# A two-layer hybrid decoder on one core: norm weights loaded in the pair's second block, weight sums a unit later, half-pass chunks a chunk sooner, query blocks scaled a step later

## The chip, the cores and the metric

The kernel runs on one core of one Trainium2 chip. The metric is device microseconds of one execution. Before the change the median of three runs is 1625.3 us (1624.74 to 1626.37). The profile is of one further execution of the same program.

## The reference

Each of two layers normalises x (512 rows of 2048), multiplies by one wide input matrix, sends the columns through three token mixers (retention, differential attention, a gated linear recurrence), multiplies each by a gate, and projects back through one output matrix. The result is normalised and added to x. All is float32. Cut to what matters:

```
for l in range(DEPTH):                                   # 2 layers
    h = rms_norm(x, pre_norm_g[l])
    proj = einsum('bsd,de->bse', h, w_in[l])
    (rq, rk, rv, rg, dq, dk, dv, dg, lx, lg) = split(proj)
    ret_out  = rms_norm(retention(rq, rk, rv)) * silu(rg)
    do       = diff_attention(dq, dk, dv, positions, lam)
    diff_out = rms_norm(do, diff_subln_g[l]) * (1 - lam_init) * silu(dg)
    lru_out  = rg_lru(lx, ...) * silu(lg)
    mixed = concatenate([ret_out, diff_out, lru_out])
    y = einsum('bse,ed->bsd', mixed, w_out[l])
    x = x + rms_norm(y, post_norm_g[l])
```

## The kernel before

**Products.** Every float32 operand is split into a high and a low part, and a product is three matmuls (high by high, high by low, low by high). A weight chunk is 128x1024 (512 KB). SP loads it as `raw` (L182), ACT copies it to `whi` (L190), DVE subtracts to `wlo` (L191). `raw`, `whi` and `wlo` have three buffers each, so a new chunk waits for the matmuls or the split that last used its buffer.

**Passes.** A layer is 13 passes over the input matrix, one pass over the first quarter of the output matrix (pass 13), the Pair, and two half passes (15 and 16) that use two of the four PSUM banks each for the last quarter. While a pass runs, `pump` takes single steps of side tasks (norms, mixers, sums) from a list, one after the other.

**The Pair** (`run_pair`, L321 to L394) computes the second and third quarter of the output in Strassen's way: seven block products, in 28 units of 12 matmuls. The order of units is A11 with chunks 0 to 3, then S1 and S3 by turns, S2 and S4 by turns, A12 and A22 by turns, four chunks each. The left-hand sums are made by `Sums`. The weights' sums are made in `load_unit` (L213 to L243): for S1 a raw chunk is loaded, DVE adds it onto the resident `wx` tiles in two halves (L230), and POOL then sends a DMA that accumulates a further block into the same raw chunk (L234), which S3 splits one unit later. S2 and A22 add a raw chunk onto `wx` in the same way; S4 and A12 use the raw chunk itself.

**Order.** SP's instructions run as the program issues them, one after the other: an issue that waits for a buffer holds all behind it. `ensure` (L246 to L254) issues a chunk's steps ahead of the matmuls: step 0 is issued LOAD = 4 chunks ahead, the rest ADD = 2 ahead or when the chunk is due. The compute engines' order is set by a scheduler with priorities; each engine runs its own list in order too.

**The rest that the change touches.** `load_chunk` (L193 to L210) is the same for the chunks of plain passes. Post-norm weights `pg` (L1186) are loaded by SP at the start of pass 13 (quarter 0), of the Pair (1 and 2) and of pass 15 (3); each takes a tile from a pool of 77. `out_y` (L1015) multiplies an output by them. In `diff_attention` (L674 to L758) a unit is a query block and a head; at a block's last head the block is squared and summed (L738), POOL takes the power (L529), and DVE scales the block (L741, L743). For the next unit DVE takes two masked maxima (L696), negates them (L699), and ACT takes the exponentials (L702).

Of the kernel before, what the change touches and what calls it, by code (L numbers as in the profile page):

```python
# [18 lines left out]
ALU = mybir.AluOpType  # L19
# [16 lines left out]
EPS = 1e-6  # L36
NU = 77
WBUFS = 3
ADD, LOAD = 2, 4
NWARM = 9  # L40
NPOOL = 4
LEAD, SLEAD, RLEAD, NLEAD = 4, 8, 6, 2
# [78 lines left out]
def tile_hybrid_trunk(ctx, tc, x, xt, pos, ppar, lamqk, w_in, gw, w_out, postg, cp, cm, out):  # L121
# [4 lines left out]
    const = ctx.enter_context(tc.tile_pool(name="const", bufs=1))  # L126
    up = ctx.enter_context(tc.tile_pool(name="up", bufs=NU))
    wp = ctx.enter_context(tc.tile_pool(name="wp", bufs=WBUFS))
    tp = ctx.enter_context(tc.tile_pool(name="tp", bufs=8))
    pb = ctx.enter_context(tc.tile_pool(name="pb", bufs=4, space=PSUM))  # L130
    pm = ctx.enter_context(tc.tile_pool(name="pm", bufs=3, space=PSUM))
    pa = ctx.enter_context(tc.tile_pool(name="pa", bufs=1, space=PSUM))
# [41 lines left out]
    chunk_list = []  # L174
    chunk_tiles = {}
    steps = {}
    loaded = [0, 0, 0]
    last_copy = [None]

    def load_raw(src):  # L180
# [12 lines left out]
    def load_chunk(i):  # L193
        p, c = chunk_list[i]
        yield
        yield
        if i:
            raw = load_raw(p.wsrc[c])
            hi, lo = split_tiles()
            split(hi, lo, raw)  # L200
        else:
            src = p.wsrc[0].rearrange("p (k c) -> p k c", k=2)
            raw = wp.tile([P, 2, S], F32, tag="raw", name=nm("raw"))
            hi, lo = split_tiles()
            for a in range(2):
                load_xt(a)
                nc.sync.dma_start(raw[:, a:a + 1, :], src[:, a:a + 1, :])
                split(hi[:, a:a + 1, :], lo[:, a:a + 1, :], raw[:, a:a + 1, :])
        chunk_tiles[i] = (hi, lo)
        yield  # L210


    def load_unit(i):  # L213
        p, (s, c) = chunk_list[i]
        w1, w2 = p.w
        if s == A11_B11:
            src = p.x[c] = [U("wx"), U("wx")]
            for kk in range(2):
                nc.sync.dma_start(src[kk], w1[c][:, kk * S:(kk + 1) * S])
        elif s == S1_T1:  # L220
            p.kept[c] = load_raw(w2[c])
        elif s == S2_T2:
            p.kept[c] = load_raw(w2[c + 4])
        elif s == A12_B21:
            p.kept[c] = load_raw(w1[c + 4])
        yield
        if s in (S1_T1, S2_T2, A22_T4):
            src = p.x[c]
            for kk in range(2):
                V.tensor_tensor(src[kk], src[kk], p.kept[c][:, kk, :], op=ALU.add)  # L230
        elif s != A11_B11:
            src = p.kept[c]
        if s == S1_T1:
            nc.gpsimd.dma_start(p.kept[c], w2[c + 4].rearrange("p (k c) -> p k c", k=2), accum_op=ALU.add)  # L234
        yield
        hi, lo = split_tiles()
        if isinstance(src, list):
            for kk in range(2):
                split(hi[:, kk, :], lo[:, kk, :], src[kk])
        else:  # L240
            split(hi, lo, src)
        chunk_tiles[i] = (hi, lo)
        yield  # L243


    def ensure(i):  # L246
        for step, more in ((0, 0), (1, 0), (2, 0), (0, ADD), (1, ADD), (0, LOAD)):
            while loaded[step] <= min(i + more, len(chunk_list) - 1):
                n = loaded[step]
                if n not in steps:  # L250
                    steps[n] = (load_unit if isinstance(chunk_list[n][0], Pair) else load_chunk)(n)
                with tc.high_priority(HP):
                    next(steps[n])
                loaded[step] += 1  # L254
# [66 lines left out]
    def run_pair(p, begin, loads):  # L321
# [48 lines left out]

        for n, (s, c) in enumerate(UNITS):
            if (s, c) in begin:
                side.append(begin[s, c]())
            if s in SUM_OF:
                until(lambda: (SUM_OF[s], c) in p.sums.parts)
            ensure(base + n + 2)
            hi, lo = chunk_tiles.pop(base + n)
            for t in range(2):
                if c == 0:
                    ps[s, t] = pb.tile([P, S], F32, tag="big", name=nm("big"))  # L380
                for kk in range(2):
                    ah, al = (stationary(s, c, kk, part)[:, t * P:(t + 1) * P] for part in range(2))
                    for m, (wt, at) in enumerate(((hi, ah), (hi, al), (lo, ah))):
                        T.matmul(ps[s, t], lhsT=at, rhs=wt[:, kk, :], start=(c == kk == m == 0),  # L384
                                 stop=(c == 3 and kk == 1 and m == 2))
                if c == 3:
                    held[s][t] = U("held")
                    with tc.high_priority(HP):
                        A.copy(held[s][t], ps.pop((s, t)))
            if n in (11, 19, 27):  # L390
                side.append({11: join_first, 19: join_right, 27: join_left}[n]())
            if n > 11:
                next(loads)
            pump()  # L394
# [279 lines left out]
    def diff_attention(l, st):  # L674
        dv = st["dv"]
        st["dod"] = {}
        units = [(i, h) for i in range(NT) for h in range(DIFF_H)]
        s0s, s1s, wts, accs, pws = {}, {}, {}, {}, {}

        def stage_a(i, h):  # L680
            n = (i + 1) * P
# [39 lines left out]
        def stage_c(i, h):  # L721
# [6 lines left out]
            if h == DIFF_H - 1:  # L728
                o = U("dod")
                V.tensor_copy(o, accs[i])  # L730
                sq = U("dsq")
                A.activation(sq, accs[i], AF.Square)
                ss = tiny("dss", 4)
                V.tensor_reduce(ss, sq.rearrange("p (h e) -> p h e", h=DIFF_H), op=ALU.add, axis=AX.X)
                r0 = tiny("r0", 4)
                V.reciprocal(r0, s0s[i])
                V.tensor_tensor(ss, ss, r0, op=ALU.mult)
                V.tensor_tensor(ss, ss, r0, op=ALU.mult)  # L738
                f = tiny("df", 4)
                rsqrt_mean(f, ss, P, 4)  # L740
                V.tensor_tensor(f, f, r0, op=ALU.mult)  # L741
                o3 = o.rearrange("p (h e) -> p h e", h=DIFF_H)
                V.tensor_tensor(o3, o3, f[:, :, None].to_broadcast([P, DIFF_H, P]), op=ALU.mult)  # L743
                st["dod"][i] = o


        A.activation(ones2, ones, AF.Exp)
# [1 line left out]
        for n in range(len(units) + 2):  # L749
            if n < len(units):  # L750
                stage_a(*units[n])
            if 0 <= n - 1 < len(units):
                stage_b(*units[n - 1])
            if 0 <= n - 2 < len(units):
                stage_c(*units[n - 2])
            yield
            if n < 4 or units[min(n, 15)][0] >= 2:
                yield  # L758

    def evac_dv(st):  # L760
        def f(tb, ps):
# [228 lines left out]
    def load_x(l, st):  # L990
        src = x2 if l == 0 else xs
        for tb in range(NT):
            for n in range(4):
# [2 lines left out]
                st["xr"][tb, n] = t  # L996
                yield

    def squares(st, tbs):
        for t in tbs:  # L1000
            for q in range(4):
# [172 lines left out]
    for l in range(DEPTH):  # L1174
# [5 lines left out]
        for i, (p, tasks) in enumerate(layer_passes[l]):  # L1180
            if i == 13:
                drain()
                side.append(st["sums"].all())
            for n in {13: (0,), 14: (1, 2), 15: (3,)}.get(i, ()):
                st["pg"][n] = U("pg")
                nc.sync.dma_start(st["pg"][n], postg[l, n * S:(n + 1) * S].partition_broadcast(P))  # L1186
            if isinstance(p, Pair):
                run_pair(p, {(S1_T1, 1): st["sums"].rest}, load_x(l, st))
            else:
                run_pass(p)  # L1190
            for t in tasks:
# [98 lines left out]
```

## Time and profile before

| what | value |
|---|---|
| median of the runs | 1625.3 us (1624.74 to 1626.37) |
| the profiled execution, its own time | 1627.36 us |
| its span | 1625.3 us |
| mean granted TensorE clock | 0.997 |
| PE busy | 1607.0 us, 99% |
| DVE busy | 1055.3 us, 65% |
| ACT busy | 713.1 us, 44% |
| POOL busy | 67.5 us, 4% |
| POOL's accumulating loads in layer 0's Pair, issued at | 675.39, 696.07, 697.30, 699.71 us |
| first and last matmul of layer 0's Pair begin | 682.44 and 762.70 us |
| first and last matmul of layer 1's Pair begin | 1489.62 and 1570.88 us |

A row of a timeline has the start in the span, the duration, the engine, the line and the operation, and in brackets the idle time before it with what ended it. A matmul's record is 0.39 us long where the next one starts 0.227 us later, so the records overlap; "PE busy" is therefore no measure of how close TensorE is to its pace, and distances between starts are. In the page's groups the columns are busy time and mean duration, then the idle time before and what ended most of it. A row of the waits has the engine and line that waited, what it waited for, the total, how often, and the longest.

### The profile page before, as it was taken

To read this page: it belongs to the slowest core of one execution; us is meant where nothing else is said; L and a number is where in the kernel's file an instruction comes from. 1 tells how busy PE (TensorE), PEld (TensorE's weight loads), DVE (VectorE), ACT (ScalarE), POOL (GpSimd) and SP (SyncE) were. 2 spreads that over 40 slices of the span, in tenths; PEclk is the share of its full clock that TensorE was granted. 3 is DMA by queue.
4 is the path that set the end of the run, shared out by engine and by line. 5 is a ranking of instruction groups with operands and counts; after the bars stand their busy time and mean duration, and the time that the engine had idled before them with its cause. 6 is when DMAs were issued, how large, how long until landed. Compare 5 with 4: busy or idle time off the path is not lost.

```text
span 1625.3 us, 19623 instructions
## 1 busy us (share of the span) xinstructions
PE 1607.0 (99%) x7445; PEld 1324.6 (81%) x7445; DVE 1055.3 (65%) x1810; ACT 713.1 (44%) x1142; POOL 67.5 (4%) x92
## 2 busy tenths in 40 slices
PE   9999999999999999999999999999999999999997
PEld 7888888888788888877888888887888888888776
DVE  7757756556586556878762774655757644467786
ACT  7233334347742224455752343435673222434452
POOL 1010000000000000000120000000000000000001
PEclk9999999999999999999999999999999999999999
DMA  6423331323232222356743233222323322233566
GB/s 231 125 89 109 95 95 61 92 84 98 78 97 90 87 72 78 116 169 200 227 152 101 92 91 103 66 85 78 98 89 93 104 65 78 91 110 116 150 207 208
DMA packets 57053, 181.70 MB, mean 112 GB/s; under 512 B 6912, under 2 KB 7936, under 8 KB 56960
## 3 DMA queue, kind: packets, MB, share of 16 engines
q1 hardware_dynamic: 53744, 169.94, 32.9%
q0 software_dynamic: 3072, 10.49, 2.5%
q8 instruction: 58, 0.95, 0.2%
q14 instruction: 35, 0.29, 0.1%
q10 hardware_dynamic: 144, 0.04, 0.0%
HBM read 172.05 MB, written 8.39 MB: 111 GB/s over the span
## 4 chain that ended last, share of the span: by engine, by line
PE 91%; DVE 3%; DMA 2%; issue 1%; ACT 1%; POOL 0%; DVEq 0%; POOLq 0%; ACTq 0%
PE big L296 78%; PE big L384 6%; DMA raw<-in_w_out 2%; DVE wlo L191 2%; PE gate L833 1%; PE acc L726 1%; PE ro L927 1%; PE rs L902 1%; PE sc L693 1%; PE sc L694 1%; ACT whi L190 1%; PE wT L716 1%; PE ro L930 0%; PE kv L916 0%; PE hT L1042 0%
## 5 line engine op out<-in xcount | busy, mean ns | idle before, releaser
L191 DVE TENSOR_TENSOR wlo<-raw,whi 128x1024 fp32r<-128x1024 f32 (+1 forms) x281 | 340.8, 1218 | 299.3 <-ACT whi L190 296.8
L190 ACT CAST whi<-raw 128x1024 fp32r<-128x1024 f32 (+1 forms) x281 | 293.4, 1048 | 473.8 <-PE big L296 313.6
L296 PE MATMUL big<-hhi,whi 128*128 128x512 f32 x1024 | 401.9, 393 | 0.0
L296 PE MATMUL big<-hhi,wlo 128*128 128x512 f32 x1024 | 399.1, 390 | 0.0
L296 PE MATMUL big<-hlo,whi 128*128 128x512 f32 x1024 | 399.1, 390 | 0.0
L296 PE MATMUL big<-whi,hhi 128*128 128x512 f32 x640 | 253.4, 398 | 0.0
L296 PE MATMUL big<-wlo,hhi 128*128 128x512 f32 x640 | 249.8, 391 | 0.0
L296 PE MATMUL big<-whi,hlo 128*128 128x512 f32 x640 | 249.8, 390 | 0.0
L296 PEld LDWEIGHTS big<-hhi,wlo 128*128 128x128 f32 x1024 | 192.2, 188 | 40.2
L296 PEld LDWEIGHTS big<-hhi,whi 128*128 128x128 f32 x1024 | 192.4, 188 | 39.6
L296 PEld LDWEIGHTS big<-hlo,whi 128*128 128x128 f32 x1024 | 192.4, 188 | 39.1
L296 PEld LDWEIGHTS big<-wlo,hhi 128*128 128x128 f32 x640 | 120.2, 188 | 25.8 <-DVE wlo L191 0.3
L296 PEld LDWEIGHTS big<-whi,hhi 128*128 128x128 f32 x640 | 120.4, 188 | 24.4 <-ACT whi L190 1.1
L296 PEld LDWEIGHTS big<-whi,hlo 128*128 128x128 f32 x640 | 120.5, 188 | 23.7
L296 PE MATMUL big<-whi,mhi 128*128 128x512 f32 x256 | 100.6, 393 | 0.7 <-ACT whi L190 0.7
L296 PE MATMUL big<-wlo,mhi 128*128 128x512 f32 x256 | 99.8, 392 | 1.0 <-DVE wlo L191 1.0
L296 PE MATMUL big<-whi,mlo 128*128 128x512 f32 x256 | 100.3, 392 | 0.0
L702 ACT ACTIVATE pr<-sc,mx 128x128 f32<-128x128 f32 (+3 forms) x64 | 33.2, 523 | 86.7 <-DVE mx L699 86.7
L296 PEld LDWEIGHTS big<-wlo,mhi 128*128 128x128 f32 x256 | 48.1, 188 | 12.1 <-DVE wlo L191 2.3
L296 PEld LDWEIGHTS big<-whi,mhi 128*128 128x128 f32 x256 | 48.1, 188 | 11.6 <-ACT whi L190 2.0
L296 PEld LDWEIGHTS big<-whi,mlo 128*128 128x128 f32 x256 | 48.1, 188 | 9.7
L384 PE MATMUL big<-whi,sh 128*128 128x512 f32 x128 | 50.7, 396 | 3.0 <-ACT whi L190 3.0
(254 smaller groups left out, 1959.8 us busy)
## 6 DMA issues: line engine op xcount, KB each, us to landing
raw<-in_w_in SPq DMA_DIRECT2D x207, 512.0 KB, 3.6
raw<-in_w_out SPq DMA_DIRECT2D x72, 512.0 KB, 4.1
xT<-in_xt SPq DMA_DIRECT2D x16, 256.0 KB, 6.6
wx<-in_w_out SPq DMA_DIRECT2D x16, 256.0 KB, 5.6
raw<-in_w_out POOLq DMA_DIRECT2D x8, 512.0 KB, 6.2
xr<-in_x SPq DMA_DIRECT2D x16, 256.0 KB, 5.5
xr<-xs SPq DMA_DIRECT2D x16, 256.0 KB, 4.8
pg<-in_postg SPq DMA_DIRECT2D x8, 256.0 KB, 4.1
```

Source lines behind the costliest of these rows:

```text
L190: last_copy[0] = A.copy(hi, raw)
L191: V.tensor_tensor(lo, raw, hi, op=ALU.subtract)
L296: T.matmul(ps[b], lhsT=lhsT, rhs=rhs, start=(cnt[b] == 0), stop=(cnt[b] == total - 1))
L384: T.matmul(ps[s, t], lhsT=at, rhs=wt[:, kk, :], start=(c == kk == m == 0), stop=(c == 3 and kk == 1 and m == 2))
L693: T.matmul(ps[:, :n], lhsT=qs[:, blk], rhs=ks[:, :n], start=True, stop=False)
L694: T.matmul(ps[:, :n], lhsT=qs[:, blk], rhs=kl[:, :n], start=False, stop=True)
L702: A.activation(p[:, :n], sc[c][:, :n], AF.Exp, bias=mx[:, c:c + 1], scale=0.125, accum_out=sums[:, h:h + 1])
L716: T.transpose(ps[:, kb * P:(kb + 1) * P], w[:, kb * P:(kb + 1) * P], ident)
L726: T.matmul(accs[i][:, h * P:(h + 1) * P], lhsT=wt[:, kb * P:(kb + 1) * P], rhs=dv[kb][:, h * P:(h + 1) * P], start=(kb == 0), stop=(kb == i))
L833: T.matmul(ps[:BW, :], lhsT=wt[:BW, cols], rhs=at[:BW, :], start=(n == 0), stop=(n == 2))
L902: T.matmul(ps[:, n * P:(n + 1) * P], lhsT=k[:, n * P:(n + 1) * P], rhs=q[:, n * P:(n + 1) * P], start=True, stop=True)
L927: T.matmul(po[:, n * P:(n + 1) * P], lhsT=sT[:, n * P:(n + 1) * P], rhs=v[:, n * P:(n + 1) * P], start=True, stop=(n == 0))
```

## The change

Four things are changed.

- The weights of quarters 1 and 2 are loaded by a function `load_gain` that the Pair calls at unit S2 with chunk 0 and at S2 with chunk 2, not both before the Pair. Quarters 0 and 3 stay.
- `load_unit` has one step more. S1's add and accumulating load stay in step 1; the adds of S2 and A22 go to step 2, which is issued one unit ahead (NEXT = 1) instead of two.
- `load_chunk` loads the raw chunk of a half pass in step 2, issued a chunk ahead; full passes load in the last step, as before.
- In `diff_attention` the end of a query block becomes a generator `stage_d`: square sum and power in one step, scaling in the next. After the last unit two steps are added for what is left, so that side tasks behind it in the list begin two steps later. The pool of small tiles has 12 buffers instead of 8.

```
-ADD, LOAD = 2, 4
+NEXT, ADD, LOAD = 1, 2, 4
...
-    tp = ctx.enter_context(tc.tile_pool(name="tp", bufs=8))
+    tp = ctx.enter_context(tc.tile_pool(name="tp", bufs=12))
...
     def load_chunk(i):
         p, c = chunk_list[i]
         yield
         yield
+        if len(p.banks) < NT:
+            raw = load_raw(p.wsrc[c])
+        yield
         if i:
-            raw = load_raw(p.wsrc[c])
+            if len(p.banks) == NT:
+                raw = load_raw(p.wsrc[c])
             hi, lo = split_tiles()
             split(hi, lo, raw)
...
     def load_unit(i):
...
         yield
-        if s in (S1_T1, S2_T2, A22_T4):
-            src = p.x[c]
+
+        def add():
             for kk in range(2):
-                V.tensor_tensor(src[kk], src[kk], p.kept[c][:, kk, :], op=ALU.add)
-        elif s != A11_B11:
-            src = p.kept[c]
+                V.tensor_tensor(p.x[c][kk], p.x[c][kk], p.kept[c][:, kk, :], op=ALU.add)
+
         if s == S1_T1:
+            add()
             nc.gpsimd.dma_start(p.kept[c], w2[c + 4].rearrange("p (k c) -> p k c", k=2), accum_op=ALU.add)
         yield
+        if s in (S2_T2, A22_T4):
+            add()
+        yield
+        src = p.x[c] if s in (A11_B11, S1_T1, S2_T2, A22_T4) else p.kept[c]
         hi, lo = split_tiles()
...
     def ensure(i):
-        for step, more in ((0, 0), (1, 0), (2, 0), (0, ADD), (1, ADD), (0, LOAD)):
+        for step, more in ((0, 0), (1, 0), (2, 0), (3, 0), (0, NEXT), (1, NEXT), (2, NEXT), (0, ADD), (1, ADD), (0, LOAD)):
...
             if h == DIFF_H - 1:
                 o = U("dod")
                 V.tensor_copy(o, accs[i])
                 sq = U("dsq")
                 A.activation(sq, accs[i], AF.Square)
-                ss = tiny("dss", 4)
...
-                st["dod"][i] = o
+                ends.append(stage_d(i, o, sq))
+
+        def stage_d(i, o, sq):
+            ss = tiny("dss", 4)
+            V.tensor_reduce(ss, sq.rearrange("p (h e) -> p h e", h=DIFF_H), op=ALU.add, axis=AX.X)
...
+            rsqrt_mean(f, ss, P, 4)
+            yield
+            V.tensor_tensor(f, f, r0, op=ALU.mult)
+            o3 = o.rearrange("p (h e) -> p h e", h=DIFF_H)
+            V.tensor_tensor(o3, o3, f[:, :, None].to_broadcast([P, DIFF_H, P]), op=ALU.mult)
+            st["dod"][i] = o
+            yield
...
                 stage_c(*units[n - 2])
+            if ends and next(ends[0], ends) is ends:
+                ends.popleft()
             yield
             if n < 4 or units[min(n, 15)][0] >= 2:
                 yield
+        while ends:
+            if next(ends[0], ends) is ends:
+                ends.popleft()
+            yield
...
+    def load_gain(l, st, n):
+        st["pg"][n] = U("pg")
+        nc.sync.dma_start(st["pg"][n], postg[l, n * S:(n + 1) * S].partition_broadcast(P))
...
-            for n in {13: (0,), 14: (1, 2), 15: (3,)}.get(i, ()):
-                st["pg"][n] = U("pg")
-                nc.sync.dma_start(st["pg"][n], postg[l, n * S:(n + 1) * S].partition_broadcast(P))
+            if i in (13, 15):
+                load_gain(l, st, 0 if i == 13 else 3)
             if isinstance(p, Pair):
-                run_pair(p, {(S1_T1, 1): st["sums"].rest}, load_x(l, st))
+                run_pair(p, {(S1_T1, 1): st["sums"].rest, (S2_T2, 0): lambda l=l, st=st: load_gain(l, st, 1),
+                             (S2_T2, 2): lambda l=l, st=st: load_gain(l, st, 2)}, load_x(l, st))
```

SP's queue at the start of layer 0's Pair, before; raw_5415 is the raw chunk of S1's chunk 0, the next three raw chunks are those of S1's chunks 1 to 3, and raw_5664 is that of S2's chunk 0:

```order
L182 DMA raw_5415<-in_w_out 128x1024
L1186 DMA pg_5515<-in_postg 128x512
L1186 DMA pg_5517<-in_postg 128x512
L182 DMA raw_5528<-in_w_out 128x1024
L182 DMA raw_5578<-in_w_out 128x1024
L182 DMA raw_5621<-in_w_out 128x1024
L182 DMA raw_5664<-in_w_out 128x1024
```

The same place in the changed kernel:

```order
L182 DMA raw_5415<-in_w_out 128x1024
L182 DMA raw_5524<-in_w_out 128x1024
L182 DMA raw_5574<-in_w_out 128x1024
L182 DMA raw_5617<-in_w_out 128x1024
L182 DMA raw_5660<-in_w_out 128x1024
L182 DMA raw_5704<-in_w_out 128x1024
L182 DMA raw_5750<-in_w_out 128x1024
L1023 DMA pg_5791<-in_postg 128x512
L182 DMA raw_5799<-in_w_out 128x1024
```

The first gain load now follows six more raw chunks, S1's 1 to 3 and S2's 0 to 2; the other one comes eight rows later, between loads of `xr`.

DVE in layer 0's Pair, before, at the splits of S3's chunks 1 and 2 (raw_1035, raw_1045 and raw_1052 hold chunks 1, 2 and 3 of S1 and S3, raw_1061 is S2's chunk 0):

```order
L230 TENSOR_TENSOR wx_999_5364<-wx_999_5364,raw_1052_5621 128x512
L230 TENSOR_TENSOR wx_1000_5365<-wx_1000_5365,raw_1052_5621 128x512
L406 TENSOR_TENSOR sl_1063_5679<-sf_969_5239,sh_1062_5678 128x512
L191 TENSOR_TENSOR wlo_1056_5638<-raw_1035_5528,whi_1055_5637 128x1024
L191 TENSOR_TENSOR wlo_1060_5656<-wx_989_5319,whi_1059_5655 128x512
L191 TENSOR_TENSOR wlo_1060_5656<-wx_990_5320,whi_1059_5655 128x512
L406 TENSOR_TENSOR sl_1067_5699<-sf_991_5335,sh_1066_5698 128x512
L191 TENSOR_TENSOR wlo_1065_5683<-raw_1045_5578,whi_1064_5682 128x1024
L406 TENSOR_TENSOR sl_1072_5725<-sf_1038_5544,sh_1071_5724 128x512
L230 TENSOR_TENSOR wx_967_5223<-wx_967_5223,raw_1061_5664 128x512
L230 TENSOR_TENSOR wx_968_5224<-wx_968_5224,raw_1061_5664 128x512
L191 TENSOR_TENSOR wlo_1069_5703<-wx_999_5364,whi_1068_5702 128x512
```

The same place in the changed kernel (there raw_1033, raw_1043 and raw_1050 hold chunks 1 to 3, and raw_1059 is S2's chunk 0):

```order
L234 TENSOR_TENSOR wx_999_5364<-wx_999_5364,raw_1050_5617 128x512
L234 TENSOR_TENSOR wx_1000_5365<-wx_1000_5365,raw_1050_5617 128x512
L191 TENSOR_TENSOR wlo_1054_5634<-raw_1033_5524,whi_1053_5633 128x1024
L416 TENSOR_TENSOR sl_1061_5675<-sf_969_5239,sh_1060_5674 128x512
L416 TENSOR_TENSOR sl_1065_5695<-sf_991_5335,sh_1064_5694 128x512
L191 TENSOR_TENSOR wlo_1058_5652<-wx_989_5319,whi_1057_5651 128x512
L191 TENSOR_TENSOR wlo_1058_5652<-wx_990_5320,whi_1057_5651 128x512
L416 TENSOR_TENSOR sl_1070_5719<-sf_1036_5540,sh_1069_5718 128x512
L416 TENSOR_TENSOR sl_1074_5741<-sf_1014_5438,sh_1073_5740 128x512
L234 TENSOR_TENSOR wx_967_5223<-wx_967_5223,raw_1059_5660 128x512
L191 TENSOR_TENSOR wlo_1063_5679<-raw_1043_5574,whi_1062_5678 128x1024
L234 TENSOR_TENSOR wx_968_5224<-wx_968_5224,raw_1059_5660 128x512
```

The add of chunk 3 (the first two rows) stands ahead of the split of S3's chunk 1 in both. The add of S2's chunk 0 stood behind the split of S3's chunk 2; half of it now stands ahead of that split. Some twenty rows up, the adds of chunks 1 and 2 stand among A11's splits now, and no longer behind the split of S3's chunk 0. Further on, the splits of S3's chunk 3 and S4's chunk 0 have an add of S2 just ahead, as they had before.

DVE in layer 0's attention where the first query block ends, before (`df` is the power, `dod` the block that is scaled, `mx` the maxima of the next unit):

```order
L528 TENSOR_SCALAR ms_2113<-dss_2106 128x4
L696 ISA sc_2131,mx_2130<-sc_2131,cmt 128x256
L696 ISA mx_2130 128x1
L741 TENSOR_TENSOR df_2112<-df_2112,r_374_2108 128x4
L696 ISA sc_2134,mx_2130<-sc_2134,cmt 128x256
L696 ISA mx_2130 128x1
L743 TENSOR_TENSOR dod_2102<-dod_2102,df_2112 128x512
L699 TENSOR_SCALAR mx_2130<-mx_2130 128x2
```

And in the changed kernel:

```order
L538 TENSOR_SCALAR ms_2113<-dss_2106 128x4
L706 ISA sc_2129,mx_2128<-sc_2129,cmt 128x256
L706 ISA mx_2128 128x1
L706 ISA sc_2132,mx_2128<-sc_2132,cmt 128x256
L706 ISA mx_2128 128x1
L756 TENSOR_TENSOR df_2112<-df_2112,r_374_2108 128x4
L709 TENSOR_SCALAR mx_2128<-mx_2128 128x2
L758 TENSOR_TENSOR dod_2102<-dod_2102,df_2112 128x512
```

The second maximum now stands ahead of the instruction that waits for the power, and the negation ahead of the scaling. In the half pass ACT's split of pass 15's chunk 1 (L190) stood behind four copies of the Pair's banks (L389) and three squares (L1008); now it stands behind one copy.

More of the change, by code (lines that the diff above doesn't have):

```diff
@@ L176, in tile_hybrid_trunk @@
     steps = {}
-    loaded = [0, 0, 0]
+    loaded = [0, 0, 0, 0]
     last_copy = [None]
@@ L372, in run_pair @@
             if (s, c) in begin:
-                side.append(begin[s, c]())
+                task = begin[s, c]()
+                if task is not None:
+                    side.append(task)
             if s in SUM_OF:
@@ L677, in diff_attention @@
         units = [(i, h) for i in range(NT) for h in range(DIFF_H)]
-        s0s, s1s, wts, accs, pws = {}, {}, {}, {}, {}
+        s0s, s1s, wts, accs, pws, ends = {}, {}, {}, {}, {}, deque()
         def stage_a(i, h):
@@ L732, in stage_c @@
                 A.activation(sq, accs[i], AF.Square)
-                ss = tiny("dss", 4)
[L734 to L743, printed above, removed]
-                st["dod"][i] = o
+                ends.append(stage_d(i, o, sq))
+        def stage_d(i, o, sq):
+            ss = tiny("dss", 4)
+            V.tensor_reduce(ss, sq.rearrange("p (h e) -> p h e", h=DIFF_H), op=ALU.add, axis=AX.X)
+            r0 = tiny("r0", 4)
+            V.reciprocal(r0, s0s[i])
+            V.tensor_tensor(ss, ss, r0, op=ALU.mult)
+            V.tensor_tensor(ss, ss, r0, op=ALU.mult)
+            f = tiny("df", 4)
+            rsqrt_mean(f, ss, P, 4)
[5 more added lines that the diff above has]
+            yield
         A.activation(ones2, ones, AF.Exp)
```

## Prediction

> **What bounds the kernel now.** I read the first part of the page, then the shares of the chain that ended last, then what TensorE waited for.
>
> ```profile
> span 1625.3 us, 19623 instructions
> PE 91%; DVE 3%; DMA 2%; issue 1%; ACT 1%; POOL 0%; DVEq 0%; POOLq 0%; ACTq 0%
> PE big L384 <- ACT whi L190: 3.0, 2, 2.1
> PE big L384 <- DVE wlo L191: 2.5, 4, 1.2
> PE big L296 <- DVE wlo L191: 1.0, 3, 0.5
> PE sc L693 <- ACT pr L702: 0.8, 2, 0.4
> PE big L296 <- ACT whi L190: 0.7, 3, 0.3
> ```
>
> TensorE makes the time: 91% of the last chain is its own work, and no edit here touches a matmul. Only its waits can be had (columns: total, times, longest). 5.5 us of them stand in the Pair (L384), 1.7 us in passes (L296), 0.8 us in the scores of the attention (L693). A wait understates its loss, because the row's length overlaps the next start; so I count starts. Timeline of PE, the Pair of both layers:
>
> ```profile
> 682.44 0.39 PE L384 MATMUL big<-whi,mhi 128*128 128x512 f32 x1
> 699.89 0.39 PE L384 MATMUL big<-wlo,sh 128*128 128x512 f32 x1
> 701.25 0.39 PE L384 MATMUL big<-wlo,sh 128*128 128x512 f32 x1
> 702.55 0.50 PE L384 MATMUL big<-whi,sh 128*128 128x512 f32 x1 [0.91 <-ACT whi L190]
> 703.81 0.50 PE L384 MATMUL big<-wlo,sh 128*128 128x512 f32 x1 [0.53 <-DVE wlo L191]
> 762.92 0.39 PE L296 MATMUL big<-whi,mhi 128*128 128x512 f32 x1
> 1489.62 0.39 PE L384 MATMUL big<-whi,mhi 128*128 128x512 f32 x1
> 1510.94 0.80 PE L384 MATMUL big<-whi,sh 128*128 128x512 f32 x1 [2.12 <-ACT whi L190]
> 1571.11 0.39 PE L296 MATMUL big<-whi,mhi 128*128 128x512 f32 x1
> ```
>
> From 682.44 to 699.89 lie 77 steps of 0.2266 us: the undisturbed pace. The Pair has 336 matmuls, so 76.1 us. From its first matmul to pass 15's first it took 80.48 us (layer 0) and 81.49 us (layer 1): it lost **4.3 and 5.4 us**. The first long stall of layer 0 is 701.25 to 702.55, less one step: 1.07 us. Two things lie behind it, on SP's timeline and in the chain of waits:
>
> ```profile
> 657.82 0.33 SPq L182 DMA_DIRECT2D raw<-in_w_out  x1
> 686.65 1.87 SPq L1186 DMA_DIRECT2D pg<-in_postg  x2
> SPq L1186 <- DVE y L1015: 56.9, 2, 28.4
> 701.45 1.05 ACT whi L190
> 703.78 5.88 DMA raw<-in_w_out
> 715.16 3.15 DMA raw<-in_w_out
> 1504.18 5.59 DMA raw<-in_w_out
> ```
>
> SP stands 28.4 us (56.9 in both layers) in front of the two gain loads, until pass 13's last y gives a tile back. Behind them in its order are the raw chunks of S1, which so start at 688.6 (686.65 + 1.87) instead of about 663. Their adds, and the accumulating loads that POOL sends after them, come late by the same; the accumulate at 1504.18 is the piece that ends just before layer 1's stall of 2.12 us.
>
> **The change part by part.**
>
> The **gain loads** go behind six raw loads (order rows of SP in the section on the change). S1's chunks 1 and 2 then need only a raw buffer, at about 663 and 668 by my estimate (buffers free as units' splits end, some 5 us apart). Their adds need the chunk of wx split, 684 to 688; accumulates go out there instead of at 696 to 700, and land before 695. The chunk of S3 that stalled at 702.55 has its data 7 us early. Its wlo stands behind the add of chunk 3, as before; that chunk's raw needs the buffer that S3's chunk 0 gives back at its split, 692.9. With the slow landing of 5.88, two adds and a split it ends by 692.9 + 5.9 + 1.3 + 1.2 = 701.3, with 701.95 wanted (unit 7's start 682.44 + 7 × 2.72, and two matmuls). Both first stalls go, and with layer 1's its slow clock. What these cost beside idle time:
>
> ```profile
> 703.00:709.00 6.00, 5.47 (x25) 4.33 (x24) 1.00 0.91 229
> 1509.00:1515.00 6.00, 4.02 (x10) 2.79 (x11) 0.72 1.04 212
> L191 DVE TENSOR_TENSOR wlo<-raw,whi 128x1024 fp32r<-128x1024 f32 (+1 forms) x281 | 340.8, 1218 | 299.3 <-ACT whi L190 296.8
> L230 DVE TENSOR_TENSOR wx<-wx,raw x48: 681/686/695, 673.5 to 1558.3; 128x512 f32<-128x512 f32 x48
> ```
>
> In the windows of the Pair's matmuls the granted clock (after the two busy times) is 1.00 after layer 0's stall and 0.72 after layer 1's; the eight starts behind 1510.94 are late by 1.9 us together. I tie these to the stall before them. The Trainium skill, "TensorE: Matmul & The Clock Gate", section "Part 1: The HAM clock gate (the "warmup" mystery)", has half rate only after about 3.4 us of idleness, in a window that runs freely. Here 2.1 us of idleness were enough, so the trace speaks against that length. By the page's rule the 1.9 us would not hang on this stall, and the sum below would be 9.3 in place of 11.2.
>
> The **later adds** of S2 and A22 stand a unit further back. This is free if raw chunk, add and split keep up with TensorE's 5.45 us for two units. A raw buffer is freed by a split, its next load takes 3.15 (alone) to 5.88 us (beside an accumulate), then half an add or both (0.6 or 1.2) and the next split of 1.22: 5.0 to 8.3 us. Only S2's first chunks can meet an accumulate, that of chunk 3 at about 699. For S3's chunk 2 I get 700 + 4.5 + 0.6 + 1.2 = 706.3, 707.4 wanted; with 5.88 it is 707.7, a stall of 0.3. The next load starts there; if it too takes 5.88, its round ends at 715.4 with 713.2 wanted, 2.2 more; if it takes 3.15, at 712.7, nothing. Bounds: 0 to 2.5 us a layer; I take 0.6, nearer to the free end, because after that one accumulate the loads are alone and the row of 3.15 is theirs. It can't be below nothing: the pace is 0.2266 already.
>
> On the rule of DMA: the 5.88 us stand beside accumulates by POOL, 3.15 alone. The Trainium skill, "DMA: Bandwidth & Descriptors", section "SWDGE vs HWDGE vs iDMA", says that software and hardware descriptors feed different internal queues of an engine, which takes turns between them. That speaks against the change, which puts raw loads beside accumulates; the row agrees. If every load of S2 met one, the third rival's time would result.
>
> The **half pass** (chunk loads a chunk sooner, and their split above the Pair's last copies in ACT's order rows):
>
> ```profile
> 765.42 0.39 PE L296 MATMUL big<-wlo,mhi 128*128 128x512 f32 x1
> 766.03 0.50 PE L296 MATMUL big<-whi,mhi 128*128 128x512 f32 x1 [0.22 <-ACT whi L190]
> 766.82 0.40 PE L296 MATMUL big<-whi,mlo 128*128 128x512 f32 x1
> 767.48 0.50 PE L296 MATMUL big<-wlo,mhi 128*128 128x512 f32 x1 [0.26 <-DVE wlo L191]
> 1575.67 0.50 PE L296 MATMUL big<-wlo,mhi 128*128 128x512 f32 x1 [0.24 <-DVE wlo L191]
> 761.03 0.57 ACT L389 COPY held<-big 128x512 f32<-128x512 f32 x1
> ```
>
> Lost: 0.61 − 0.23 = 0.38 and 0.66 − 0.23 = 0.43, and by an equal wait (1575.67) the same in layer 1: **1.6 us**. ACT held this split back behind four copies and three squares; now one copy is ahead, so it needs only its buffer and by my estimate ends some 4 us sooner than 766.0, against a wait of 0.2. The copies that fall behind it are later by one split of ACT (some 1.05 us, the row at 701.45); the first of their banks was free at 761.6 and is wanted six matmuls behind pass 15's first, at 764.3. The last pass's own stalls at the program's end (the third of "x3" in both rows) keep their order and stay.
>
> The **query block's scaling**:
>
> ```profile
> 258.05 0.39 PE L296 MATMUL big<-hlo,whi 128*128 128x512 f32 x1
> 258.85 0.38 PE L693 MATMUL sc<-st,st 128*128 128x256 f32 x1 [0.42 <-ACT pr L702]
> 255.97 1.02 POOL df L529
> 257.58 0.55 DVE dod L743
> 258.12 0.09 DVE mx L699
> PE rsb L587 <- DVE rb L586: 0.3, 1, 0.3
> PE gate L833 <- ACT xh L818: 0.2, 1, 0.2
> ```
>
> DVE waited for POOL's power (to 257.0) ahead of the second maximum, then scaled 0.55 us, then negated the maximum that ACT's exponential needs. In the new order both maxima stand before that wait and the negation before the scaling: it moves from 258.1 to about 257.2, 0.9 us, against 0.80 − 0.23 = 0.57 us lost, once a layer ("0.8, 2" in the waits above): **1.15 us**. Two added steps at the attention's end push gates and heads back by 24 matmuls, 5.4 us. The largest waits of PE for gates and heads are 0.3 and 0.2 us (last two rows); I cost the shift at nothing, and such a wait gone or come at ± 0.5. Tables on ACT go from 26 loads to 22, beside idle time.
>
> **Sum**: 4.3 + 5.4 + 1.6 + 1.15 = 12.4, less 2 × 0.6 left in S2: **11.2 us**. The profiled execution took 1627.4 us in all (2.1 around its span), so 1616.2 for it; the median of the runs, 1625.3, is 2.1 below it, so **1614.1**.
>
> **The rivals.**
>
> 1. The loop of raw load, add and split binds in S2. For it: 5.88, and stalls that layer 0 had behind the first, which sum to 4.3 − 1.07 = 3.2. Against: one accumulate only is left there. At its upper bound of 2.5 us a layer the gain is 12.4 − 5.0 = 7.4: 1617.9.
> 2. The gain loads only move the wait: the new place waits for a tile too, and holds what is queued behind. For it: 28.4 us for a tile at the old place. Against: pass 13's last y is by then 10 us past. The Pair then keeps its 9.7, and 1.6 + 1.15 = 2.8 remain: 1622.5, which is within 0.2%.
> 3. Slower. The adds of late raw chunks stand ahead of the splits of S3 on DVE, as its order rows show, and DVE can't pass them. If each of chunks 1 to 3 lands as slowly as the row of 5.88, a round takes 0.03 + 5.9 + 1.2 + 1.2 = 8.3 against 5.45: 2.9 × 3, less some 2.2 of slack, 6.5 a layer, and a slow clock of 1.9 with it: 8.4 a layer for the 4.3 and 5.4 lost now, +7.1, less 2.8: 1629.6. It costs more than before from a landing of 5.2 us in all three: 3 × (5.2 − 3.0) − 2.2 + 1.9 = 6.3 a layer, half of the 12.4 now lost. Against: chunks 1 and 2 have 20 us more to land, and only one accumulate is left beside the rest.
> 4. The clock falls in the Pair whatever the stall (the page's rule, above): 1.9 less: 1616.0. For it: only 2.1 us of idleness came before. Against: layer 0, 1.00 with its 0.9 and 0.5 us.
>
> **How the numbers follow.** Forecast (1612.5 to 1615.7) 0.53, rival 4 0.05, rival 1 (to 1619.5) 0.22, rival 2 0.08, rival 3 0.05; 0.07 for something between 1619.5 and 1622. The range of 8 in 10 reaches from the lower bound (nothing left in S2, and 0.5 of side work: 1614.1 − 1.7) to rival 1's with a slow clock of 1.9 on top: 1612.4 to 1619.8. Within 0.2% (3.25 us) is about what a measurement here can't tell from none, so faster is below 1622.05: 0.86; same 0.09; slower 0.05.
>
> **What would show it.** SP's gain loads after S2's start, raw loads of S1's chunks 1 and 2 before 672; POOL's accumulates before 690; the stalls at 702.5 and 1510.9 gone with a clock of 1.00; the waits L296 by one each; the L693 row gone; the Pair 76.2 to 77.5 us long. Wrong would be: a wait by DVE for a raw chunk ahead of an S3 split (rival 1 or 3), a stall that reappears in the gates and heads which moved 5.4 us.

## The result

Four runs of the changed kernel have a median of 1616.15 us (1615.81 to 1617.22), four of the kernel before 1625.84 us (1624.74 to 1627.07): a ratio of 0.9941 with a 95% interval of 0.9924 to 0.9959. That is 9.7 us, or 0.6%, faster. Forecast were 1614.1 us and a gain of 11.2 us. The time lies in the stated range, 2 us above the forecast.

### The profile page after: what moved, and what is told of

The parts are those of the page before. It is cut to its first block, busy times and chain, and to the rows that moved or that the text cites. A ratio compares the mean times of both kernels' runs of the same rounds, so it can differ in the third digit from the quotient of the medians.

```text
span 1613.8 us, 19637 instructions
## 1 busy us (share of the span) xinstructions
PE 1602.5 (99%) x7445; PEld 1324.9 (82%) x7445; DVE 1053.7 (65%) x1810; ACT 709.1 (44%) x1138; POOL 67.6 (4%) x92
## 4 chain that ended last, share of the span: by engine, by line
PE 95%; DVE 2%; DMA 1%; ACT 1%; issue 1%; POOL 0%; DVEq 0%; POOLq 0%; ACTq 0%
PE big L304 79%; PE big L394 8%; PE gate L855 1%; DVE wlo L191 1%; PE acc L736 1%; DMA raw<-in_w_out 1%; PE ro L949 1%; PE rs L924 1%; PE sc L703 1%; PE sc L704 1%; PE ro L952 0%; PE kv L938 0%; PE wT L726 0%; PE hT L1068 0%; PE rT L979 0%
## 5 line engine op out<-in xcount | busy, mean ns | idle before, releaser
L191 DVE TENSOR_TENSOR wlo<-raw,whi 128x1024 fp32r<-128x1024 f32 (+1 forms) x281 | 341.4, 1218 | 285.7 <-ACT whi L190 282.8
L190 ACT CAST whi<-raw 128x1024 fp32r<-128x1024 f32 (+1 forms) x281 | 293.7, 1048 | 468.4 <-PE big L304 305.2
L304 PE MATMUL big<-hhi,whi 128*128 128x512 f32 x1024 | 401.9, 393 | 0.0
L304 PE MATMUL big<-hlo,whi 128*128 128x512 f32 x1024 | 399.4, 390 | 0.0
L304 PE MATMUL big<-hhi,wlo 128*128 128x512 f32 x1024 | 399.0, 390 | 0.0
L304 PE MATMUL big<-whi,hhi 128*128 128x512 f32 x640 | 253.5, 398 | 0.0
L304 PE MATMUL big<-whi,hlo 128*128 128x512 f32 x640 | 249.9, 391 | 0.0
L304 PE MATMUL big<-wlo,hhi 128*128 128x512 f32 x640 | 249.7, 391 | 0.0
L304 PEld LDWEIGHTS big<-hhi,whi 128*128 128x128 f32 x1024 | 192.4, 188 | 40.6 <-ACT qk L680 0.9
L304 PEld LDWEIGHTS big<-hhi,wlo 128*128 128x128 f32 x1024 | 192.2, 188 | 40.2
L304 PEld LDWEIGHTS big<-hlo,whi 128*128 128x128 f32 x1024 | 192.4, 188 | 38.7
L304 PEld LDWEIGHTS big<-wlo,hhi 128*128 128x128 f32 x640 | 120.2, 188 | 25.7
L304 PEld LDWEIGHTS big<-whi,hhi 128*128 128x128 f32 x640 | 120.5, 188 | 23.9 <-ACT whi L190 0.7
L304 PEld LDWEIGHTS big<-whi,hlo 128*128 128x128 f32 x640 | 120.6, 188 | 23.8
L304 PE MATMUL big<-wlo,mhi 128*128 128x512 f32 x256 | 100.2, 392 | 0.5 <-DVE wlo L191 0.5
L304 PE MATMUL big<-whi,mhi 128*128 128x512 f32 x256 | 100.3, 392 | 0.1
L304 PE MATMUL big<-whi,mlo 128*128 128x512 f32 x256 | 100.2, 391 | 0.0
L304 PEld LDWEIGHTS big<-wlo,mhi 128*128 128x128 f32 x256 | 48.1, 188 | 10.9 <-DVE wlo L191 1.0
L304 PEld LDWEIGHTS big<-whi,mhi 128*128 128x128 f32 x256 | 48.1, 188 | 10.2 <-ACT whi L190 0.5
L304 PEld LDWEIGHTS big<-whi,mlo 128*128 128x128 f32 x256 | 48.1, 188 | 9.7
L190 ACT CAST whi<-wx 128x512 fp32r<-128x512 f32 x64 | 37.1, 619 | 38.8 <-PE big L394 28.8
```

The lines of the kernel that those rows point to most:

```text
L190: last_copy[0] = A.copy(hi, raw)
L191: V.tensor_tensor(lo, raw, hi, op=ALU.subtract)
L304: T.matmul(ps[b], lhsT=lhsT, rhs=rhs, start=(cnt[b] == 0), stop=(cnt[b] == total - 1))
```

## The profile after

The profiled execution took 1615.81 us with a span of 1613.8 us; the one before took 1627.36 us. The page, the chain's shares and all that TensorE waited for in passes, Pair and scores:

```profile
span 1613.8 us, 19637 instructions
PE 95%; DVE 2%; DMA 1%; ACT 1%; issue 1%; POOL 0%; DVEq 0%; POOLq 0%; ACTq 0%
PE big L304 <- DVE wlo L191: 0.5, 1, 0.5
PE big L394 <- DVE wlo L191: 0.4, 1, 0.4
PE sc L703 <- ACT pr L712: 0.3, 2, 0.2
```

Lines have moved: L394 is the Pair (L384 before), L304 the passes (L296), L703 the scores (L693), L182 and L191 are as they were. The Pair's waits went from 5.5 us in six waits to one of 0.4, the passes' from 1.7 to 0.5 (the program's last pass), the scores' from 0.8 to 0.3. Timeline of PE around the Pairs:

```profile
682.25 0.39 PE L394 MATMUL big<-whi,mhi 128*128 128x512 f32 x1
707.72 0.50 PE L394 MATMUL big<-wlo,sh 128*128 128x512 f32 x1 [0.38 <-DVE wlo L191]
759.38 0.39 PE L304 MATMUL big<-whi,mhi 128*128 128x512 f32 x1
1484.63 0.39 PE L394 MATMUL big<-whi,mhi 128*128 128x512 f32 x1
1560.81 0.39 PE L304 MATMUL big<-whi,mhi 128*128 128x512 f32 x1
```

First matmul to pass 15's first is 77.13 us in layer 0 (80.48 before) and 76.18 in layer 1 (81.49), against 76.15 at the undisturbed pace. From profile to profile the Pairs gave 3.4 and 5.3 us. What SP and POOL issued in layer 0's Pair:

```profile
657.63 55.46 SPq L182 DMA_DIRECT2D raw<-in_w_out  x7
713.14 0.42 SPq L1023 DMA_DIRECT2D pg<-in_postg  x1
686.01 0.90 POOL L238 DMA_DIRECT2D raw<-in_w_out  x1 [9.73 <-ACT whi L190]
688.37 0.87 POOL L238 DMA_DIRECT2D raw<-in_w_out  x1 [1.47 <-ACT whi L190]
697.89 0.87 POOL L238 DMA_DIRECT2D raw<-in_w_out  x1 [8.65 <-ACT sh L415]
```

The gain load stands behind seven raw loads and waits for nothing worth a row; the accumulates of chunks 1 and 2 start at 686 and 688 instead of 696 and 697, that of chunk 3 at 698 instead of 700.

## The experiments

Each was made from the kernel before (the first four) or from the changed one, with five rounds against the kernel before; runs of one group shared a chip. Before had a median of 1624.71 us in the first group, 1625.46 in the second, 1625.70 in the third.

### The four parts, each alone

```
 # e1_gain: kernel before, and
-            for n in {13: (0,), 14: (1, 2), 15: (3,)}.get(i, ()):
+            if i in (13, 15):
+                load_gain(l, st, 0 if i == 13 else 3)
...
+                run_pair(p, {(S1_T1, 1): st["sums"].rest, (S2_T2, 0): lambda l=l, st=st: load_gain(l, st, 1),
+                             (S2_T2, 2): lambda l=l, st=st: load_gain(l, st, 2)}, load_x(l, st))
 # e2_adds: kernel before, and in load_unit
+        if s in (S2_T2, A22_T4):     # in a step of its own, a unit later
+            add()
 # e3_half: kernel before, and in load_chunk
+        if len(p.banks) < NT:
+            raw = load_raw(p.wsrc[c])
+        yield
 # e4_diff: kernel before, and diff_attention of the changed one, with 12 small tiles
```

> Only the gain loads move (into S2); adds, half passes and attention as before. Theory: SP's 28 us wait before S1's raw chunks is the cause of the first long stall of each Pair. S1's raw loads start before 672 us, the stalls at 702.5 (2.0 us with what follows it) and 1510.9 (2.4, and 1.9 of slow clock) are gone, the later ones of 715 to 739 stay: Pair of layer 0 78.4 us long (80.5 before), of layer 1 77.2 (81.5). Time 4.4 us below before where before's execution had no slow clock (median about 1621.4), 6.3 below where it had one. Rival: the order of the adds on DVE binds and the waits only come back one chunk later; then the Pairs stay within 0.7 us of 80.5 and 81.5 and the time within 1.5 us of before.

> Only the adds of S2 and A22 come a unit later; the gain loads stay before the Pair. Theory: the first long stall of each Pair stays (702.5 and 1510.9, SP blocked for 28 us), at most the later ones go: gain between 0 and 2 us. Rival: the adds are what shortens the Pair, SP's wait was hidden: Pairs of 77.1 and 76.2 us as with the whole change, gain about 7 us.

> Only the half-pass chunks are loaded a chunk sooner. Theory: the four stalls at 766.0, 767.5, 1574.2 and 1575.7 go, 1.6 us, and the Pairs stay at 80.5 and 81.5 us: 1624.2 against 1625.8. Rival: ACT's order there came from the Pair's earlier end and not from this edit; then the four stalls stay and the gain is under 0.3 us.

> Only the query block's end is a step later. Theory (from the profile of the whole change): the wait of the score matmuls falls from 0.8 to 0.3 us in total, since the negated maximum still stands behind the instruction that waits for POOL's power: gain 0.5 us, not 1.15. Rival of the prediction: both stalls go entirely, gain 1.15 us. A third: the shift of gates and heads by 24 matmuls costs or brings over 0.5 us by itself, visible in stalls between 345 and 425 and between 1110 and 1185 us.

| run | median us | ratio to before | Pair, layer 0 and 1, in its profile |
|---|---|---|---|
| gain loads alone | 1619.14 | 0.9964 (0.9951 to 0.9976) | 77.2, 77.4 us |
| later adds alone | 1625.42 | 1.0002 (0.9993 to 1.0011) | 79.6, 79.2 us |
| half passes alone | 1622.86 | 0.9985 (0.9976 to 0.9994) | 80.0, 80.0 us |
| query blocks alone | 1624.71 | 0.9997 (0.9988 to 1.0007) | 79.2, 80.0 us |

The gain loads are the larger part of the change: alone they bring 0.36 of 0.59%, and the Pairs fall to 77.2 and 77.4 us (78.4 and 77.2 were expected). In layer 0 that is more than expected: the later stalls between 715 and 739, which were to stay, are gone as well. In the profile of the later adds alone SP stands before the gain loads as it did, and the chain of waits has the same pieces, raw landing, adds, accumulate, split, up to the stall:

```profile
659.55 0.33 SPq L182 DMA_DIRECT2D raw<-in_w_out  x1
688.39 1.86 SPq L1008 DMA_DIRECT2D pg<-in_postg  x2
1496.71 6.03 DMA raw<-in_w_out
1502.77 1.30 DVE wx L231 x2
1504.62 5.15 DMA raw<-in_w_out
1509.85 1.05 ACT whi L190
```

The rows are SP's timeline and, from 1496 on, the chain. Without the gain loads' move the later adds bring nothing that the runs can tell; the interval ends 1.1 us below before, far from the rival's 7. The half passes alone lose the four stalls, as their waits show (of the three waits in each row of L296 one is left, that of the last pass), and bring 1.9 us (interval 1.0 to 3.9) where 1.6 was summed:

```profile
PE big L303 <- DVE wlo L191: 0.5, 1, 0.5
PE big L303 <- ACT whi L190: 0.4, 1, 0.4
```

The query block's edit more than halves the waits, alone as in the whole (0.8 to 0.3 us in all); in time it can't be told from nothing, nor from the 1.15 us of the prediction. Multiplied, the four ratios give 0.9948, so no large interaction is needed for the whole's 0.9941.

### The whole again, and without the later adds

```
 # e5_whole: the changed kernel.   e6_no_adds: the changed kernel, and in load_unit
-        if s == S1_T1:
+        if s in (S1_T1, S2_T2, A22_T4):
             add()
...
-        if s in (S2_T2, A22_T4):
-            add()
```

> The whole change again, beside the next three on one chip. Theory (the parts seen apart: gain loads 5.6, half passes 1.9, attention 0 to 0.5, later adds nothing alone): 8 to 10 us below before. The prediction's 11.2 holds the 1.9 us of slow clock that only some executions of before have. Rival: 11.2 us, the parts simply worth what the one profile showed.

> The whole change without the later adds (S2 and A22 as before). Theory: once the gain loads are out of the way, the later adds are worth the stalls that the gain loads alone left at 709.8 (0.8) and 1513.8 (1.1): 0.5 to 2 us slower than the whole change, Pairs of about 77.2 and 77.4 us. Rival: the adds' place does nothing; then the same as the whole change within 0.3 us, and the Pairs 77.1 and 76.2.

The whole: 1616.75 us, ratio 0.9948 (0.9935 to 0.9960), 8.7 us below before, as expected; the interval, 6.5 to 10.6 us, leaves out the rival's 11.2. Without the later adds: 1616.71 us, 0.9944 (0.9931 to 0.9958), with Pairs of 77.3 and 76.2 us (77.4 and 76.3 in the whole of this group). My theory fell: the later adds make no difference that the runs can tell, neither alone nor on top; the intervals leave room for some 2 us, but the Pairs agree within 0.1. DVE has the same order here: the add of S2's chunk 0 begins at 706.25, the split of S3's chunk 2 behind it at 706.86, and TensorE stalls at 708.13 as in the whole. The stall of 1.1 us that the gain loads alone had left in layer 1 is not there, though the adds are issued as they were: so it is not due to their place. What made it stays open.

### What is left in layer 0: hold the accumulate, or take the adds off DVE

Chain of the changed kernel before the stall at 707.72, then DVE's timeline there:

```profile
697.27 1.23 DVE wlo L191
698.52 7.30 DMA raw<-in_w_out
706.45 1.23 DVE wlo L191
705.84 0.69 DVE L234 TENSOR_TENSOR wx<-wx,raw 128x512 f32<-128x512 f32 x1 [3.73 <-DMA raw<-in_w_out]
706.45 1.22 DVE L191 TENSOR_TENSOR wlo<-raw,whi 128x1024 fp32r<-128x1024 f32 x1
```

S2's chunk 0 is loaded at 698.52, just behind the accumulate that POOL sent at 697.89, and takes 7.30 us. Its add stands at DVE's head for 3.73 us; the split of S3's chunk 2 stands behind it. Two edits separate landing and order.

```
 # e7_hold: the changed kernel, and in load_unit, S1's chunk 3 accumulates only after this
+            zero, one = tiny("hold", 1), p.kept[3][:, 0, :1]
+            G.tensor_tensor(zero, p.kept[0][:, 0, :1], p.kept[0][:, 0, :1], op=ALU.subtract)
+            G.tensor_tensor(one, one, zero, op=ALU.add)
 # e8_both: as e7_hold, and e9_behind: the changed kernel, each with this in stage_d
-            V.tensor_tensor(f, f, r0, op=ALU.mult)
+            V.scalar_tensor_tensor(r1, newest[0][:, :1].to_broadcast([P, 4]), 0.0, r0, op0=ALU.mult, op1=ALU.add)
+            V.tensor_tensor(f, f, r1, op=ALU.mult)
 # e10_pool_adds: as e9_behind, and in load_unit for S2 and A22
-            add()
+            add(G)
```

> The whole change, with the accumulating load of S1's chunk 3 held back on POOL until S2's chunk 0 has landed (POOL adds a difference of that chunk with itself, zero, to one column of the other first). Theory: the 7.3 us landing of S2's chunk 0 in layer 0 comes from the accumulate beside it; it falls to 3.2 to 4.0, the stalls at 707.7 and 735.2 (0.9 us) go, layer 0's Pair is 76.2 to 76.5 us long, gain 0.6 to 0.9 us on the whole change. Rival: the landing is slow for another reason (its issue, the splits): it stays above 5.5 us and the Pair at 77.1; or the accumulate, now later, keeps S3's chunk 3 waiting and costs over 0.5 us.

> As the run before, and the factor of a query block is tied behind the negated maximum of the next unit (zero times that maximum is added to it), so that the negation no longer stands behind the wait for POOL's power. Theory: the two score stalls left (0.32 us each) go too: 0.6 us below the run before, 1.2 to 1.6 below the whole change. Rival: the place of the score matmuls on TensorE sets the stall, and it stays at 0.3 each; or the four added instructions a layer cost as much.

> The whole change, and the factor of a query block is tied behind the next unit's negated maximum (zero times that maximum is added to it); no hold on the accumulate. Theory: the two score stalls of 0.32 us go, 0.6 us below the whole change (1616 to 1616.8): 1615.4 to 1616.2. Rival: the run before won its 1.1 us by chance of the clock; then no difference from the whole change, with the stalls gone or not.

> As the run before, and the adds of S2 and A22 run on POOL instead of DVE. Theory: the stall of layer 0's Pair that the whole change leaves (0.5 to 0.9 us at 707.7) comes from the add of S2's chunk 0 that stands at the head of DVE, waiting for a raw chunk that lands late beside the accumulate, while the split of S3's chunk 2 behind it is ready since 702.3. Without that add on DVE the stall goes, the landing of 6 to 7 us stays: Pair of layer 0 76.2 to 76.4 us, 0.9 us more gained. Rival: POOL's adds take so long, or slow DVE so much, that S2's or A22's own splits come late: Pairs of 77.5 us or more.

**Holding the accumulate** gave 1620.67 us, 0.9970 (0.9959 to 0.9982): 3.9 us slower than the whole. The rival's second half came: the later accumulate keeps S3's chunk 3 waiting. Layer 0's Pair is 79.9 us long where 76.2 to 76.5 were expected. Its chain:

```profile
699.97 4.73 DMA raw<-in_w_out
706.90 6.68 DMA raw<-in_w_out
713.68 1.05 ACT whi L190
714.76 1.24 DVE wlo L191
```

Without the accumulate beside it the raw chunk lands in 4.73 us instead of 7.30 (3.2 to 4.0 were expected), and the stall at 707.7 is gone. So the hold took 2.6 us off the landing; why it still takes 4.73 us and not 3.15, as a load alone in the prediction, stays open. The accumulate itself, sent at 706.90, takes 6.68 us and now makes S3's chunk 3 late: 1.2 and 0.7 us of stall at 714.8 and 716.0, and a slow clock behind them (0.79 from 716 to 724).

**The negation freed** from the wait for POOL's power. On top of the hold: 1619.61 us, 0.9964 (0.9951 to 0.9976), 1.1 below it, which the intervals don't tell apart. On the whole change alone: 1616.42 us, 0.9946 (0.9933 to 0.9958), where the whole had 0.9948. The row of the scores is gone from the waits of both profiles; the 0.6 us that the two stalls had lost is too little to be told in time from the whole change.

**The adds on POOL** gave 1620.54 us, 0.9971 (0.9960 to 0.9983), 4.1 us slower than the run beside it that has the adds on DVE. The rival came: the Pairs are 80.3 and 78.4 us long (77.7 and 76.2 beside it). The stall at 707.7 is gone: without the add at its head DVE splits S3's chunk 2 at 702.16, right behind ACT's copy, and not at 706.45. That shows that the add's place made that stall, and not the chunk's own data. But POOL takes 1.80 us for an add that takes DVE 0.69, and DVE's own work beside it slows down. POOL's adds are busy until 742.1, a new stall of 2.4 us by starts ends at 742.7 with a slow clock behind it, and a like one of 2.1 us comes in layer 1. DVE's timeline at that split, the group of POOL's adds, then DVE's timeline before the new stall, and the stall:

```profile
702.16 1.23 DVE L191 TENSOR_TENSOR wlo<-raw,whi 128x1024 fp32r<-128x1024 f32 x1 [0.17 <-ACT whi L190]
L234 POOL TENSOR_TENSOR wx<-wx,raw 128x512 f32<-128x512 f32 x32 | 56.8, 1800 | 29.9 <-DMA raw<-in_w_out 17.6 <-PE big L394 7.9 <-DVE held L351 2.4
737.51 1.77 DVE L191 TENSOR_TENSOR wlo<-wx,whi 128x512 fp32r<-128x512 f32 x1
739.21 1.78 DVE L357 TENSOR_TENSOR held<-held,held 128x512 f32<-128x512 f32 x1
742.57 0.68 DVE L358 TENSOR_TENSOR held<-held,held 128x512 f32<-128x512 f32 x1
742.70 0.50 PE L394 MATMUL big<-wlo,mhi 128*128 128x512 f32 x1 [2.23 <-DVE wlo L191]
```

No version beat the whole change by a margin that the runs can tell.

### Two more profiles of the kernel before

Nothing is edited; each is one look at the kernel before.

> The kernel before once more, unchanged, for a second profile of it. Theory: the stall that starts layer 1's trouble at 1510.9 is there again (1.3 to 2.3 us), but the slow clock behind it (1.9 us) comes only in some executions and in others falls elsewhere or nowhere; the Pair of layer 1 is then some 79.6 us long. Rival: it belongs to the stall and is there each time: 81.5.

> The same once more: a third profile of the kernel before. Expected as in the run before it.

| profile of before | time us | Pair layer 0 | Pair layer 1 | first stall of layer 1 |
|---|---|---|---|---|
| first (of the prediction) | 1627.36 | 80.48 us | 81.49 us | idle 2.12 us |
| second | 1626.09 | 79.76 us | 79.85 us | idle 1.00 and 0.53 us |
| third | 1625.56 | 80.48 us | 80.07 us | idle 1.25 and 0.53 us |

The theory fell, though not to the rival either: the slow clock in layer 1's Pair is in all three, as windows around it show (first, second, third; then layer 0's first stall in the second; then layer 1's stretch in the changed kernel):

```profile
1509.00:1517.00 8.00, 6.02 (x19) 4.42 (x20) 4.77 (x6) 5.74 (x9) 0.00 (x0) 0.79 0.95 217
1509.00:1517.00 8.00, 6.47 (x20) 4.55 (x19) 5.62 (x8) 5.79 (x9) 0.00 (x0) 0.79 0.96 239
1509.00:1517.00 8.00, 6.23 (x20) 4.64 (x20) 5.69 (x8) 5.83 (x9) 0.00 (x0) 0.79 0.95 241
703.00:709.00 6.00, 4.53 (x19) 3.44 (x20) 4.77 (x6) 5.67 (x9) 0.00 (x0) 1.00 0.98 231
1503.00:1511.00 8.00, 8.00 (x37) 6.63 (x36) 5.16 (x8) 3.59 (x5) 0.00 (x0) 1.00 0.54 136
```

The columns are the window, its length, the busy times of PE, PE's loads, DVE, ACT and POOL, then the granted clock (0.79 three times, then 1.00), the DMA share and GB/s. What varied were the stalls: 81.49 us was the longest of three Pairs, the others are 1.6 and 1.4 us shorter. The first stall makes 0.4 and 0.2 of that (by starts it lost 2.28, 1.86 and 2.11 us), and 0.7 is a further stall that only the first profile has:

```profile
1546.95 0.50 PE L384 MATMUL big<-wlo,sh 128*128 128x512 f32 x1 [0.56 <-DVE wlo L191]
```

Nor is the slow clock there whenever the stall is: the profiles of the later adds alone and of the query blocks alone have the stall in layer 1 (2.3 and 2.1 us lost) and a clock of 1.00 behind it.

## Why the prediction was right, and where it was off

**The gain loads** (4.3 and 5.4 us of the sum): right in mechanism and place. SP's raw loads run from 657.6, the accumulates of chunks 0 to 2 have gone out by 688.4, both first stalls and layer 1's slow clock are gone. Of the sum's terms this one was mis-sized most: the 5.4 us of layer 1 were those of one execution, with a longer first stall and a further one at 1546.95. The two later profiles of before lose 79.85 − 76.15 = 3.7 and 3.9 us there. With 3.8 in place of 5.4 the sum is 9.6 us, with the query block's 0.5 in place of 1.15 (below) 9.0; the gains measured by medians are 9.7 and 8.7 us (the whole, twice), with intervals of some 2 to 3 us on either side. The step that carried it over was "so 1616.2 for it; the median of the runs, 1625.3, is 2.1 below it, so 1614.1": the profiled execution of before was the longest of the runs then known, and its long Pair of layer 1 was counted whole as gain. From profile to profile the fall was 11.5 us; the kernel's was less.

**The later adds**: costed at a loss of 0 to 2.5 us a layer, 0.6 taken. What is left in the Pairs is 1.0 us in layer 0 and nothing in layer 1, 1.0 in all against 1.2. But that loss is not theirs: it stays when the adds go back to their old place, so that the sizes match is luck. The cause is the one named, a raw load beside an accumulate (7.30 us, more than the 5.88 that was the upper bound), at the place named, S3's chunk 2, and it is the third rival's mechanism in one chunk: an add at the head of DVE before a split that is ready. The prediction had named just this, a wait by DVE for a raw chunk ahead of an S3 split, as a sign of being wrong; it came, but in one layer and for 0.5 to 1.1 us in the profiles of the whole and of its variants that keep this order, not for the rival's 6.5 and more.

**The half passes** (1.6 us): right. In the whole and alone all four stalls are gone.

**The query block** (1.15 us): the direction was right, the size less than half: the stalls fell by 0.5 us in all, and the row of the scores, which was to be gone, stayed with 0.3. The order was read on DVE alone. The negation did move 0.9 us forward, but the score matmuls moved too: before, 1,073 matmuls of the passes stand ahead of the one that stalls in layer 0, now 1,070, three steps of 0.227 us sooner. Timeline of PE and DVE after:

```profile
257.22 0.39 PE L304 MATMUL big<-hlo,whi 128*128 128x512 f32 x1
257.77 0.38 PE L703 MATMUL sc<-st,st 128*128 128x256 f32 x1 [0.16 <-ACT pr L712]
256.87 0.16 DVE L756 TENSOR_TENSOR df<-df,r 128x4 f32<-128x4 f32 x1 [0.44 <-POOL df L539]
256.95 0.16 DVE L709 TENSOR_SCALAR mx<-mx 128x2 f32<-128x2 f32 x1
```

From 257.22 to 257.77 is 0.55, less a step 0.32: of 0.57 us lost, 0.25 was won, once a layer. The negation at 256.95 still stands behind the instruction that waits for POOL; freeing it removed the rest.

**The clock**: rival 4, that it falls whatever the stall, is not borne out: with the stalls gone the clock is 1.00 in the Pairs of all four profiles of the whole and of its variants that have no stall of over 1.1 us. That its 1616.0 us is the number nearest to the measured 1616.15 is chance, since the shortfall has the causes above. Nor does the stall's length settle it: layer 0's stall of the second profile of before is as long as layer 1's (1.2 and 0.7 us lost in both) and its clock stays 1.00 (window from 703 above). Against the length of idleness that "TensorE: Matmul & The Clock Gate" of the Trainium skill states (section "Part 1: The HAM clock gate (the "warmup" mystery)", about 3.4 us), half rate came after 1.00 and 0.53 us; that its window runs freely fits that equal stalls end differently.

The traces show where the difference lies. In each profile the clock changes only at points that lie whole multiples of 3.413 us apart: in the second profile of before it falls at 41.29 and at 1512.43, which are 431 such steps, and each fall between start and end lasts one step. Windows of this grid in that profile, over and behind layer 0's stall, then over and behind layer 1's:

```profile
703.47:706.89 3.42, 2.42 (x9) 1.72 (x10) 2.97 (x5) 3.36 (x6) 0.00 (x0) 1.00 1.06 207
706.89:710.30 3.41, 3.41 (x16) 2.82 (x15) 1.80 (x3) 1.84 (x4) 0.00 (x0) 1.00 0.87 280
1509.02:1512.43 3.41, 1.88 (x7) 0.97 (x6) 2.04 (x3) 3.12 (x5) 0.00 (x0) 1.00 1.03 195
1512.43:1515.84 3.41, 3.41 (x9) 2.65 (x9) 2.73 (x4) 2.08 (x5) 0.00 (x0) 0.50 0.91 251
```

Layer 0's stall is cut by an edge of the grid, so only 1.17 us of it are lost in one window; layer 1's 1.86 us fall into one window, and the next is at half rate. Over the Pairs of all fourteen profiles, seven windows lost 1.86 to 2.39 us to stalls, and half rate followed each; no other window at full rate lost more than 1.80, and none was followed by half rate. This was read from the traces afterwards and no run tests it; the gap between 1.80 and 1.86 is narrow.

**Gates and heads**, moved by 24 matmuls: the gate's wait of 0.2 us is gone from the waits after, another (`rsb`, 0.3 us) fell to 0.2, and none of over 0.2 came; they cost nothing that a wait shows.

## What to carry to other kernels

A queue that issues in order pays for its slowest waiter: two loads of 256 KB, first used some 65 us later, held back a chain of load, add, accumulate and split, and moving them behind what is needed first was most of the gain. A stall read from one execution is a sample: look at a second profile before counting its whole length, above all where a slow clock or a landing beside other transfers is part of it. And read a moved instruction on both sides: the one that waits may move as well.

## What the runs showed of the hardware that was not expected

A slow clock comes to the same program in some executions and not in others. In the start-up phase of the kernel before, second profile and third, windows from 41 to 46 us:

```profile
41.00:46.00 5.00, 5.00 (x17) 3.77 (x16) 2.37 (x9) 0.23 (x1) 1.03 (x1) 0.66 0.82 265
41.00:46.00 5.00, 4.77 (x22) 3.50 (x22) 3.09 (x10) 0.69 (x1) 1.03 (x1) 1.00 0.77 241
```

At a granted clock of 0.66, 17 matmuls start in these 5 us where 22 do otherwise. No stall like those of the Pair stands before it (TensorE is busy 3.37 of the 3.41 us ahead); what brings it stays open. Of the 48 timed runs of the kernel before in these three groups the shortest took 1622.38 us and the longest 1627.79: differences of a microsecond between two kernels need many runs. And adds on POOL slowed DVE beside them: the same 128x512 operation on held tiles took 1.78 us at 739 and, with POOL done, 0.68 at 742.6.
